# Group B softmax of a two-layer streaming encoder: a chained row minimum, a plain scale that ScalarE may do, and the factor 1/2 put into the output weights

## The chip, the cores and the metric

The kernel runs on one core of one Trainium2 chip. A core has TensorE (PE in the profile, with its weight loads as PEld), VectorE (DVE), ScalarE (ACT), GpSimd (POOL), SyncE (SP), which issues the DMAs, an on-chip memory (SBUF) that all of them read, and a smaller one (PSUM) that TensorE writes. The metric is device time in microseconds (us) for one execution, lower is better; a figure without further words is the median of three runs.

## The reference

Two layers of a streaming encoder, one inference step for 2048 prompt frames and 32 sample frames, model width 1024, all in fp32. What matters here is layer 0. One projection gives two attention groups; each group's output is multiplied by its own SiLU gate, the two are concatenated, and one output projection follows.

```python
def ab_output(oa, ob, ga, gb, w_out):
    y = jnp.concatenate([oa.reshape(b, t, -1) * jax.nn.silu(ga),
                         ob.reshape(b, t, -1) * jax.nn.silu(gb)], axis=-1)
    return y @ w_out

def attend(q, k, v, q_pos, k_pos, valid, bias_table, sinks):
    s = einsum(q, k) * (dh ** -0.5)
    if bias_table is not None: s = s + bias          # group B
    s = where(valid, s, -1e30)
    if sinks is not None:                            # group A
        m = maximum(max(s), sink); p = exp(s - m); p = p / (sum(p) + exp(sink - m))
    else:
        p = softmax(s)                               # group B
    return einsum(p, v)
```

Group A looks back two chunks of 64 frames, with 8 query heads on 2 key heads and a learned sink; group B looks back eight chunks, with 8 heads and a learned bias by distance. Layer 1 (projection, short convolution, linear recurrence, output projection) comes after all of layer 0. Of silu(g) = g * sigmoid(g) the kernel computes g * (1 + tanh(g/2)), which is twice silu(g). The missing factor 1/2 has to be applied somewhere, and this is one of the things that the change moves.

## The kernel before

Every large matrix product is done as three products of fp32r parts: a weight tile `wst` of 128x1024 is split into a rounded part `wh` and a rest `wl`, the activations into `r0h` and `r0l` (or `r1h`, `r1l`), and TensorE adds r0h*wh, r0l*wh and r0h*wl into one PSUM tile `acc`. These dense products are most of TensorE's work.

The order of all instructions is set when the program is built. The kernel holds its own list scheduler (`Sched`): each piece of work is a Python generator that yields a request `R(engines, inputs, rings, cost)`; the scheduler keeps an estimated time for each engine, gives a request to the engine that would finish it first by the costs written there, and records the instruction in that order. On the chip each engine then runs its list strictly in order and waits on semaphores. A request with several engines, such as ("V", "G"), lets the scheduler choose among VectorE (V), GpSimd (G) and ScalarE (A). Attention work has priority on TensorE; where none is ready, the dense products of `dense_P` (input projection) and later `dense_2` (output projection, then layer 1) fill in. So a change of one cost or of one instruction moves much that comes after it.

Layer 0 has three blocks of tokens. Attention for the tiles of a block runs between the dense products of the next ones; the last block's attention lies under the first third of the output projection, and the other output blocks wait for the key `("attention",)`.

A tile of group B attention has 128 queries and up to 640 keys, and goes through these steps, in the functions `soft`, `transp` and `evac_B`:

1. TensorE computes the scores into PSUM tiles `S` (two matmuls a bank, with the rounded query parts `qa` and `qb`). 640 keys don't fit into one bank of 512, so there are two banks of 320, that is two entries of `groups`.
2. VectorE runs one fused instruction for each bank (`reduce`; in the profile CUSTOM_DVE_ANT_0): it adds the bias, changes the sign, writes `pt` in SBUF and keeps the row minimum, which a second short instruction (DVE_READ_ACCUMULATOR2_ANT; in the built order both are named ISA) writes to a column of `nm`.
3. With two banks, a further VectorE instruction on two columns of 128x1 takes the smaller of the two minima (`nm<-nm`). There are 96 of them for prompt tiles and 8 for the sample.
4. ScalarE computes exp(-pt + nm) over all 640 columns, with the row sum into `ssm`; VectorE takes its reciprocal into `rr`.
5. VectorE or GpSimd multiplies `pt` by `rr` and by 0.5 (`pt<-pt,rr`).
6. TensorE transposes `pt` block by block into PSUM tiles `T`; ScalarE writes the rounded copy and VectorE the rest into `pp`; TensorE multiplies `pp` by the values `vt` into `O`; ScalarE and VectorE add the parts into `ot`, and a DMA writes it out.

Group A goes the same way with four heads beside each other; its fused instruction starts from the sink (operand `nsk`), so it has no step 3.

The output projection's weights (named "wo0" in `WSEQ`, 8 tiles for each of the 3 blocks) are split like all others, by `w_split`: `wh` on ScalarE or VectorE, `wl` on VectorE or GpSimd.

Of the kernel before, what the change touches and what calls it, by code (L numbers as in the profile page):

```python
# [11 lines left out]
AF = mybir.ActivationFunctionType  # L12
OP = mybir.AluOpType
# [42 lines left out]
def f32(ap):  # L56
    return ap.bitcast(F32)
# [341 lines left out]
def hybrid_kernel(ctx, tc, I, O):  # L399
# [85 lines left out]
    def w_split():  # L485
        for i in range(1, len(WSEQ)):
# [6 lines left out]
            s = wst.pop(i)  # L493
            if e == "A":
                A.copy(h, s)
            else:
                V.tensor_copy(h, s)
            e, _ = yield R(("V", "G"), [h], cost=(1.14, 2.3))
            ENG[e].tensor_tensor(l, s, f32(h), OP.subtract)
            wstr.release(s)  # L500
# [730 lines left out]
    def soft(run, np_, groups, out, sink=None):  # L1231
# [9 lines left out]

        def reduce(ps, pieces, o0):
            yield R("V", [ps] + ex)
            o = 0
            for i, (_, ks, bv, j) in enumerate(pieces):
                n = ks.stop - ks.start
                V.tensor_tensor_reduce(out=pt[:np_, o0 + o:o0 + o + n], in0=ps[:np_, o:o + n], in1=bv, scale=-1.0,
                                       scalar=BIG if sink is None else nsk[:np_, sink + j:sink + j + 1],
                                       op0=OP.add, op1=OP.min, accum_out=nm[:np_, j:j + 1])
                o += n  # L1250
            Sr.release(ps)
            left[0] -= 1
            if not left[0]:
                if run.bias is not None:
                    run.b_done()
                if sink is None and len(groups) == 2:
                    V.tensor_tensor(nm[:np_, 0:1], nm[:np_, 0:1], nm[:np_, 1:2], OP.min)
                if sink is not None:
                    V.tensor_tensor(r[:np_], sk[:np_, sink:sink + 4], nm[:np_], OP.add)
                sch.set(uid, sch.t["V"] + 0.13)  # L1260

        for gi, pieces in enumerate(groups):
# [5 lines left out]
            for qs, ks, _, _ in pieces:  # L1268
# [3 lines left out]
                o += n  # L1272
            spawn(reduce(ps, pieces, o0), PT)
            o0 += o
# [14 lines left out]
        n = sum(x[1] for x in out)  # L1289
        e, _ = yield R(("V", "G"), [r], cost=(0.06 + n * 0.00053, 0.1 + n * 0.00106))  # L1290
        for j, (o, w) in enumerate(out):
            x = pt[:np_, o:o + w]
            ENG[e].tensor_scalar(x, x, r[:np_, j:j + 1], 0.5, OP.mult, OP.mult)
        for g, t in ((nmr, nm), (smr, ss), (rr4, r)):
# [827 lines left out]
```

## Time and profile before

| what | value |
| --- | --- |
| median of 3 runs | 1827.37 us (1827.22 to 1828.31) |
| the profiled execution's own time | 1823.5 us |
| span of that execution, first to last instruction | 1821.7 us |
| TensorE busy | 1731.5 us, 95% of the span |
| VectorE busy | 1555.3 us, 85% |
| ScalarE busy | 996.5 us, 55% |
| GpSimd busy | 326.5 us, 18% |
| mean share of the full TensorE clock that was granted | 0.988 |
| first and last score minimum that is taken from two banks | 412.8 and 989.9 us |

The profile is of one execution, and its times count from the first instruction. Almost all instructions pass through one helper, so they all stand at line L101; the names of the tiles tell them apart (out<-in, buffer numbers left out). A busy time counts an instruction from its start to its end, and on TensorE and VectorE one starts before the one before it has ended, so the distance between two starts is what an instruction costs its engine. "Idle before" is the engine's idle time just before an instruction, with what ended it; gaps under 150 ns aren't counted.

### The profile page before, as it was taken

Reading aid. Unit: us, or ns where it says so; the run is one execution under the profiler, and the core shown is the slowest. Engines: PE = TensorE matmul, PEld = TensorE weight load, DVE = VectorE, ACT = ScalarE, POOL = GpSimd, SP = SyncE. Lnnn points to the kernel's source line nnn. Section 1 sums busy time; section 2 is a strip of 40 time slices with the busy share of each in tenths; the row PEclk is TensorE's granted clock in tenths of the full one; section 3 lists DMA queues with packets and bytes.
Section 4 is the critical chain, followed back from the end, with each engine's and each line's share of the span. In section 5 each row is a group of like instructions: output and inputs, shape, how many; then the busy total and the mean of one; then the engine's idle time right before and its main releaser. Section 6 shows DMA issues by size and latency. Waiting matters only on the chain.

```text
span 1821.7 us, 31694 instructions
## 1 busy us (share of the span) xinstructions
PE 1731.5 (95%) x11078; PEld 1671.8 (92%) x11078; DVE 1555.3 (85%) x3330; ACT 996.5 (55%) x2037; POOL 326.5 (18%) x284
## 2 busy tenths in 40 slices
PE   8999999999999999999998999998999999999995
PEld 7999999998999999899997999998999899999995
DVE  9899967899998779998988789899999988798843
ACT  4275543476666416665565344457753675447831
POOL 4332204323322233311222000000011000100002
PEclk8999999999999999999998999999999999999998
DMA  5788766888654368877764985684566735575376
GB/s 179 203 245 265 228 190 196 226 232 237 192 149 141 97 186 248 210 217 195 216 194 122 278 248 168 210 267 147 217 213 217 204 124 174 165 208 171 128 268 193
DMA packets 293576, 362.80 MB, mean 199 GB/s; under 512 B 36308, under 2 KB 244616, under 8 KB 293400
## 3 DMA queue, kind: packets, MB, share of 16 engines
q1 hardware_dynamic: 293416, 360.78, 66.5%
q8 instruction: 87, 1.43, 0.3%
q14 instruction: 73, 0.60, 0.1%
HBM read 255.77 MB, written 107.00 MB: 199 GB/s over the span
## 4 chain that ended last, share of the span: by engine, by line
PE 49%; DVE 29%; DMA 9%; ACT 6%; issue 4%; SPq 1%; POOL 1%; DVEq 0%; ACTq 0%; POOLq 0%
PE acc L101 35%; PE T L101 4%; PE O L101 4%; PE S L101 4%; DVE pt L101 3%; DVE ex L101 3%; DVE m L101 3%; DMA xr<-x2T 3%; DVE ss L101 2%; DVE ti L101 2%; DVE xs L101 2%; DVE s L101 2%; DVE pp L101 2%; DVE eti L101 1%; DVE wl L101 1%
## 5 line engine op out<-in xcount | busy, mean ns | idle before, releaser
L101 PE MATMUL acc<-r0h,wh 128*128 128x352 f32 (+2 forms) x1832 | 592.1, 323 | 6.7 <-ACT tzb L101 2.9
L101 PE MATMUL acc<-r0h,wl 128*128 128x352 f32 (+2 forms) x1832 | 592.2, 323 | 2.9 <-DMA wl<-wo1s 2.9
L101 PE MATMUL acc<-r0l,wh 128*128 128x352 f32 (+2 forms) x1832 | 592.5, 323 | 0.6 <-DVE r0l L101 0.5
L101 PEld LDWEIGHTS acc<-r0h,wh 128*128 128x128 f32 x1832 | 346.2, 189 | 9.3 <-ACT tzb L101 3.1
L101 PEld LDWEIGHTS acc<-r0h,wl 128*128 128x128 f32 x1832 | 346.3, 189 | 4.8 <-DMA wl<-wo1s 4.0
L101 PEld LDWEIGHTS acc<-r0l,wh 128*128 128x128 f32 x1832 | 346.4, 189 | 2.2 <-DVE r0l L101 1.2
L101 PE MATMUL acc<-r1h,wh 128*128 128x352 f32 (+1 forms) x864 | 277.5, 321 | 5.2 <-ACT tz L101 3.6
L101 PE MATMUL acc<-r1h,wl 128*128 128x352 f32 (+1 forms) x864 | 277.0, 321 | 1.6 <-DVE wl L101 1.6
L101 PE MATMUL acc<-r1l,wh 128*128 128x352 f32 (+1 forms) x864 | 276.9, 321 | 0.0
L101 ACT ACTIVATE pt<-pt,nm 128x256 f32<-128x256 f32 (+6 forms) x272 | 169.8, 627 | 61.2 <-DVE nm L101 59.3
L101 ACT CAST pp<-T 128x256 fp32r<-128x256 f32 (+4 forms) x314 | 134.0, 438 | 84.3 <-PE T L101 65.8
L101 PEld LDWEIGHTS acc<-r1h,wh 128*128 128x128 f32 x864 | 162.3, 188 | 6.4 <-ACT tz L101 4.5
L101 POOL TENSOR_SCALAR pt<-pt,rr 128x256 f32<-128x256 f32 (+4 forms) x142 | 100.2, 716 | 366.4 <-DVE rr L101 217.0
L101 PEld LDWEIGHTS acc<-r1h,wl 128*128 128x128 f32 x864 | 162.3, 188 | 1.9 <-DVE wl L101 1.9
L101 PEld LDWEIGHTS acc<-r1l,wh 128*128 128x128 f32 x864 | 162.3, 188 | 0.0
L101 PE MATMUL T<-ident,pt 128*128 128x128 f32 (+2 forms) x864 | 143.3, 274 | 18.0 <-DVE pp L101 10.2
L101 DVE TENSOR_TENSOR pp<-T,pp 128x256 fp32r<-128x256 f32 (+4 forms) x314 | 150.4, 496 | 7.9 <-ACT pp L101 6.0
L101 PE MATMUL O<-pp,vt 128*128 128x256 f32 (+3 forms) x728 | 135.9, 310 | 9.8 <-DVE pp L101 4.7
L101 PEld LDWEIGHTS T<-ident,pt 128*128 128x128 f32 (+2 forms) x864 | 101.7, 140 | 42.4 <-DVE pp L101 19.9
L101 DVE CUSTOM_DVE_ANT_0 pt<-S,bias 128x320 f32<-128x320 f32 (+2 forms) x240 | 108.8, 478 | 17.4 <-PE S L101 14.6
L101 PE MATMUL S<-kk,qa 128*128 128x320 f32 (+5 forms) x376 | 119.7, 333 | 3.8 <-DVE nm L101 3.3
L101 PEld LDWEIGHTS O<-pp,vt 128*128 128x128 f32 (+1 forms) x728 | 107.1, 193 | 16.0 <-DVE pp L101 6.1
(241 smaller groups left out, 3010.1 us busy)
## 6 DMA issues: line engine op xcount, KB each, us to landing
wst<-w_in SPq DMA_DIRECT2D x93, 512.0 KB, 4.4
wst<-wo_in SPq DMA_DIRECT2D x32, 512.0 KB, 5.6
wh<-w1s SPq DMA_DIRECT2D x32, 512.0 KB, 3.8
wl<-w1s SPq DMA_DIRECT2D x32, 512.0 KB, 4.6
wh<-wo1s SPq DMA_DIRECT2D x24, 512.0 KB, 3.9
wl<-wo1s SPq DMA_DIRECT2D x24, 512.0 KB, 4.7
kk<-kB SPq DMA_DIRECT2D x32, 320.0 KB, 4.8
vt<-vB SPq DMA_DIRECT2D x16, 640.0 KB, 4.8
```

Of the source, the lines that this page charges most:

```text
L101: r = fn(*a, **k)
```

## The change

Three edits:

- **The chained minimum.** In group B the second bank's fused instruction starts its minimum from the first bank's result (column 1 of `nm`, as a scalar operand) and writes column 0. The separate minimum of step 3 is gone. The second bank's instruction now waits for the first bank's minimum to be written.
- **The plain scale.** Step 5 multiplies by `rr` alone. Where one instruction covers the whole tile (group B), ScalarE may do it too, at an estimated cost of 0.197 us + n/1200.
- **The factor 1/2.** It goes into the split of the "wo0" tiles: `wh` is 0.5 times the weight, and `wl` is 0.5 times the weight minus `wh`, one fused VectorE instruction; GpSimd may no longer do it for these 24 tiles.

```diff
@@ w_split
+            half = WSEQ[i][0] == "wo0"
+            if half:
+                if e == "A":
+                    A.activation(h, s, AF.Copy, scale=0.5)
+                else:
+                    V.tensor_scalar(h, s, 0.5, None, OP.mult)
+                yield R("V", [h])
+                V.scalar_tensor_tensor(l, s, 0.5, f32(h), OP.mult, OP.subtract)
             else:
-                V.tensor_copy(h, s)
-            e, _ = yield R(("V", "G"), [h], cost=(1.14, 2.3))
-            ENG[e].tensor_tensor(l, s, f32(h), OP.subtract)
...
@@ soft
-        def reduce(ps, pieces, o0):
-            yield R("V", [ps] + ex)
+        def reduce(ps, pieces, o0, gi):
+            on = gi > 0 and sink is None
+            yield R("V", [ps] + ex + ([(uid, 0)] if on else []))
...
+                if sink is None:
+                    j = len(groups) - 1 - gi
                 V.tensor_tensor_reduce(out=pt[:np_, o0 + o:o0 + o + n], in0=ps[:np_, o:o + n], in1=bv, scale=-1.0,
-                                       scalar=BIG if sink is None else nsk[:np_, sink + j:sink + j + 1],
+                                       scalar=nsk[:np_, sink + j:sink + j + 1] if sink is not None else nm[:np_, 1:2] if on else BIG,
                                        op0=OP.add, op1=OP.min, accum_out=nm[:np_, j:j + 1])
...
-                if sink is None and len(groups) == 2:
-                    V.tensor_tensor(nm[:np_, 0:1], nm[:np_, 0:1], nm[:np_, 1:2], OP.min)
...
-        e, _ = yield R(("V", "G"), [r], cost=(0.06 + n * 0.00053, 0.1 + n * 0.00106))
+        e, _ = yield R(("V", "G", "A")[:3 if len(out) == 1 else 2], [r], cost=(0.06 + n * 0.00053, 0.1 + n * 0.00106, 0.197 + n / 1200.0))
...
-            ENG[e].tensor_scalar(x, x, r[:np_, j:j + 1], 0.5, OP.mult, OP.mult)
+            if e == "A":
+                A.activation(x, x, AF.Copy, scale=r[:np_, j:j + 1])
+            else:
+                ENG[e].tensor_scalar(x, x, r[:np_, j:j + 1], None, OP.mult)
```

Since the scheduler plans anew, the built order of every engine differs from there on. Three places show what moves. In the rows, the numbers at the names are buffers; `x3` is three equal instructions in a row.

VectorE, the first pair of banks in the program (in block 1). Before:

```order
L101 ISA pt_211,nm_216<-S_194,bias_207 128x320
L101 ISA nm_216 128x1
L101 ISA pt_211,nm_216<-S_195,bias_207 128x320
L101 ISA nm_216 128x1
L101 TENSOR_TENSOR nm_216<-nm_216 128x1
L101 TENSOR_TENSOR ot_214<-O_198,ot_214 64x512
```

And now:

```order
L101 ISA pt_211,nm_216<-S_194,bias_207 128x320
L101 ISA nm_216 128x1
L101 ISA pt_211,nm_216<-S_195,bias_207,nm_216 128x320
L101 ISA nm_216 128x1
L101 TENSOR_TENSOR ot_214<-O_198,ot_214 64x512
```

The minimum is gone, and the second bank's instruction reads `nm`. In all, 104 minima go; in 71 of the 104 pairs the second instruction stands right behind the first's minimum, and in the others something stands between.

ScalarE, the first such tiles of block 1 (exp of a tile, then the copies of transposed tiles). Before:

```order
L101 ACTIVATE pt_210,ssm_222<-pt_210,nm_218 128x640
L101 CAST pp_212<-T_196 128x2x128
L101 COPY ot_215<-O_198 64x512
L101 CAST pp_212<-T_197 128x3x128
L101 CAST pp_213<-T_196 128x3x128
L101 ACTIVATE pt_211,ssm_223<-pt_211,nm_219 128x640
```

And now:

```order
L101 ACTIVATE pt_210,ssm_222<-pt_210,nm_218 128x640
L101 ACTIVATE pt_210<-pt_210,rr_226 128x640
L101 CAST pp_212<-T_197 128x2x128
L101 CAST pp_212<-T_196 128x3x128
L101 COPY ot_215<-O_198 64x512
```

A scale by `rr` now stands in ScalarE's list, ahead of copies out of `T`. Of the scales of 640 columns GpSimd had 57 and VectorE 39; now GpSimd has 28, VectorE 43 and ScalarE 25. With the shorter ones ScalarE has 33.

TensorE, a pair of group B tiles of one of the last heads of the last block, from the last tile's first transposes to the end of `O` (the dense products between them are `acc`). Before:

```order
L101 MATMUL T_196<-ident,pt_209 128x128 x3
L101 MATMUL acc_159<-r0l,wh_121 128x324
L101 MATMUL acc_159<-r0h,wl_124 128x324
L101 MATMUL acc_159<-r0h,wh_121 128x324
L101 MATMUL acc_159<-r0l,wh_121 128x324
L101 MATMUL O_198<-pp_212,vt_206 128x2x128 x4
L101 MATMUL acc_159<-r0h,wl_124 128x324
L101 MATMUL acc_159<-r0h,wh_121 128x324
L101 MATMUL acc_159<-r0l,wh_121 128x324
L101 MATMUL acc_159<-r0h,wl_124 128x324
L101 MATMUL O_198<-pp_212,vt_206 128x2x128 x4
L101 MATMUL O_198<-pp_212,vt_206 128x256 x2
```

And now:

```order
L101 MATMUL T_196<-ident,pt_209 128x128 x3
L101 MATMUL O_198<-pp_212,vt_206 128x2x128 x4
L101 MATMUL acc_158<-r0h,wh_121 128x352
L101 MATMUL acc_158<-r0l,wh_121 128x352
L101 MATMUL acc_158<-r0h,wl_124 128x352
L101 MATMUL acc_158<-r0h,wh_121 128x352
L101 MATMUL O_198<-pp_212,vt_206 128x2x128 x4
L101 MATMUL O_198<-pp_212,vt_206 128x256 x2
```

Four dense matmuls between the transposes and the first `O` are gone from here and come later. Over the program TensorE's 11061 matmuls stay the same; the last one of attention was the 6291st and is now the 6163rd, so 128 dense matmuls that stood before the end of attention now stand behind it. Nearly all of that is in the attention of the last block.

Beyond these, the 24 splits of "wo0" tiles use the new instructions. VectorE now does all 24 rests, and over all weights GpSimd has 37 rests of 128x1024 and had 39.

More of the change, by code (lines that the diff above doesn't have):

```diff
@@ L493, in w_split @@
             s = wst.pop(i)
-            if e == "A":
-                A.copy(h, s)
-            else:
-                V.tensor_copy(h, s)
-            e, _ = yield R(("V", "G"), [h], cost=(1.14, 2.3))
-            ENG[e].tensor_tensor(l, s, f32(h), OP.subtract)
+            half = WSEQ[i][0] == "wo0"
[6 more added lines that the diff above has]
+                V.scalar_tensor_tensor(l, s, 0.5, f32(h), OP.mult, OP.subtract)
+            else:
+                if e == "A":
+                    A.copy(h, s)
+                else:
+                    V.tensor_copy(h, s)
+                e, _ = yield R(("V", "G"), [h], cost=(1.14, 2.3))
+                ENG[e].tensor_tensor(l, s, f32(h), OP.subtract)
             wstr.release(s)
@@ L1251, in reduce @@
             Sr.release(ps)
+            sch.set((uid, gi), sch.t["V"])
             left[0] -= 1
@@ L1272, in soft @@
                 o += n
-            spawn(reduce(ps, pieces, o0), PT)
+            spawn(reduce(ps, pieces, o0, gi), PT)
             o0 += o
@@ L1289, in soft @@
         n = sum(x[1] for x in out)
-        e, _ = yield R(("V", "G"), [r], cost=(0.06 + n * 0.00053, 0.1 + n * 0.00106))
+        e, _ = yield R(("V", "G", "A")[:3 if len(out) == 1 else 2], [r], cost=(0.06 + n * 0.00053, 0.1 + n * 0.00106, 0.197 + n / 1200.0))
         for j, (o, w) in enumerate(out):
             x = pt[:np_, o:o + w]
-            ENG[e].tensor_scalar(x, x, r[:np_, j:j + 1], 0.5, OP.mult, OP.mult)
+            if e == "A":
+                A.activation(x, x, AF.Copy, scale=r[:np_, j:j + 1])
+            else:
+                ENG[e].tensor_scalar(x, x, r[:np_, j:j + 1], None, OP.mult)
         for g, t in ((nmr, nm), (smr, ss), (rr4, r)):
```

## The prediction

> **What bounds the kernel now.** I read the page's totals first, then the stretches of time in the last block's attention, where the built order moves most. The columns of a stretch are its length, then for each engine the busy time and the instructions, then the granted TensorE clock, the DMA share and GB/s.
>
> ```profile
> PE 1731.5 (95%) x11078; PEld 1671.8 (92%) x11078; DVE 1555.3 (85%) x3330; ACT 996.5 (55%) x2037; POOL 326.5 (18%) x284
> ...
> 840.00:900.00 60.00, 59.48 (x416) 56.84 (x416) 54.37 (x170) 35.98 (x84) 10.90 (x8) 1.00 0.74 207
> 900.00:960.00 60.00, 57.02 (x396) 54.13 (x395) 53.69 (x157) 35.31 (x79) 18.19 (x11) 1.00 0.73 196
> 960.00:1000.00 40.00, 34.66 (x212) 31.89 (x213) 32.71 (x89) 23.07 (x53) 10.04 (x6) 0.87 0.40 123
> 1000.00:1040.00 40.00, 40.00 (x256) 40.00 (x255) 28.12 (x37) 15.82 (x30) 0.94 (x1) 1.00 0.85 257
> ```
>
> TensorE is the bound: 1731.5 of 1821.7 us, and nothing in this change takes a matmul away. So the change can only touch the 90.2 us in which TensorE is idle, and time that its clock is low. VectorE comes next: 54 of 60 us in these stretches, so a delay there is soon a delay of TensorE. From 960 to 1000 TensorE loses 5.3 us idle and has 0.87 of its clock, another 40 x 0.13 = 5.2 us; right after attention it is full.
>
> Next, what TensorE's idle time waits for between 780 and 1000 us (groups of instructions there), and the start and end of the `O` matmuls in the whole program (rows of the tile `pp`):
>
> ```profile
> L101 PE MATMUL T<-ident,pt 128*128 128x128 f32 (+1 forms) x277 | 47.1, 273 | 6.7 <-DVE pp L101 4.2 <-DMA vt<-vBs 1.1 <-POOL pt L101 0.9
> L101 PE MATMUL O<-pp,vt 128*128 128x256 f32 (+2 forms) x273 | 43.3, 292 | 3.2 <-DVE pp L101 1.8 <-DMA vt<-vBs 1.3
> L101 PE MATMUL S<-kk,qa 128*128 128x320 f32 (+1 forms) x106 | 36.7, 354 | 0.6 <-DVE nm L101 0.6
> ...
> L101 PE MATMUL O<-pp,vt x728: 193/283/582, 95.3 to 1002.0; 128*128 128x256 f32 x141, 128*128 128x512 f32 x31, 128*128 128x64 f32 x8, 32*128 32x64 f32 x2
> ```
>
> That is 10.5 us in 220 us, 6.0 of it ended by VectorE's writing of `pp` and 0.6 by `nm`. Then I looked at what stood ahead of `pp` on VectorE, at the longest such wait (timeline of VectorE, GpSimd, TensorE and ScalarE from 957 us: start, length, instruction):
>
> ```profile
> 957.66 0.48 DVE L101 CUSTOM_DVE_ANT_0 pt<-S,bias 128x320 f32<-128x320 f32 x1
> 958.07 0.08 DVE L101 DVE_READ_ACCUMULATOR2_ANT nm<- 128x1 f32 x1
> 958.18 1.75 DVE L101 TENSOR_TENSOR nm<-nm 128x1 f32<-128x1 f32 x1
> 959.86 0.87 DVE L101 TENSOR_TENSOR pp<-T,pp 128x256 fp32r<-128x256 f32 x2
> ...
> 957.56 2.36 POOL L101 TENSOR_TENSOR wl<-wst,wh 128x1024 fp32r<-128x1024 f32 x1
> ...
> 960.32 0.44 PE L101 MATMUL T<-ident,pt 128*128 128x128 f32 x2 [1.66 <-DVE pp L101]
> ...
> 960.03 0.83 ACT L101 ACTIVATE pt<-pt,nm 128x640 f32<-128x640 f32 x1 [3.11 <-DVE nm L101]
> ```
>
> A minimum of one column takes 1.75 us. It ends at 959.93, as GpSimd's 2.36 us instruction does (959.92): it waited for it. `pp` waits behind it, and TensorE idles 1.66 us for `pp`. The fused instruction ran through the same GpSimd instruction in its usual 0.48 us. The chain of waits, by line, says how often this decides (100 and 200 us):
>
> ```profile
> by line: PE acc L101 24.1%; DVE pt L101 12.0%; DVE pp L101 9.8%; DVE ss L101 7.8%; DVE ot L101 6.2%; PE T L101 5.8%; issue 5.7%; PE S L101 5.1%; PE O L101 5.0%; DMA oT<-ot 4.6%; DVE nm L101 4.0%; DVE xt L101 3.3%; PE misc L101 1.5%; DVE sr
> ...
> by line: PE acc L101 19.8%; PE O L101 9.5%; DVE pt L101 9.2%; DMA vt<-vBs 8.5%; PE T L101 8.0%; PE S L101 7.3%; DMA xt<-zT 6.1%; DVE ot L101 5.6%; DVE pp L101 4.4%; DVE nm L101 3.7%; issue 3.5%; DVE r0l L101 2.0%; DVE xt L101 1.8%; DVE s L1
> ```
>
> The first is 400 to 500 us, the second 800 to 1000 us: `nm` has 4.0 and 7.4 us on the chain, 11.4 together.
>
> **The change, part by part.** The minimum undisturbed, and the groups by form:
>
> ```profile
> 437.05 0.08 DVE L101 DVE_READ_ACCUMULATOR2_ANT nm<- 128x1 f32 x1
> 437.17 0.16 DVE L101 TENSOR_TENSOR nm<-nm 128x1 f32<-128x1 f32 x1
> 437.24 0.15 DVE L101 RECIPROCAL rr<-ssm 128x1 f32<-128x1 f32 x1
> ...
> L101 DVE TENSOR_TENSOR nm<-nm x104: 147/159/1815, 412.8 to 989.9; 128x1 f32<-128x1 f32 x96, 32x1 f32<-32x1 f32 x8
> ...
> L101 DVE TENSOR_TENSOR nm<-nm 128x1 f32<-128x1 f32 x96 | 30.8, 321 | 3.3
> L101 DVE CUSTOM_DVE_ANT_0 pt<-S,amask,nsk 128x256 f32<-128x256 f32 x120 | 51.6, 477 | 2.9 <-PE S L101 2.5
> L101 DVE CUSTOM_DVE_ANT_0 pt<-S,bias 128x256 f32<-128x256 f32 x8 | 3.3, 414 | 0.0
> L101 DVE TENSOR_TENSOR wl<-wst,wh 128x1024 fp32r<-128x1024 f32 x86 | 110.8, 1288 | 2.8 <-ACT wh L101 0.8
> L101 DVE TENSOR_SCALAR pt<-pt,rr 128x640 f32<-128x640 f32 x39 | 24.5, 633 | 0.7
> L101 POOL TENSOR_SCALAR pt<-pt,rr 128x640 f32<-128x640 f32 x57 | 55.2, 970 | 237.1 <-DVE rr L101 146.1 <-ACT pp L101 39.0 <-PE O L101 13.3
> L101 ACT ACTIVATE pt<-pt,nm 128x640 f32<-128x640 f32 x96 | 79.9, 832 | 37.4 <-DVE nm L101 35.8 <-DVE pp L101 1.2
> ```
>
> The minimum, removed: from the end of the bank's own work (437.05) to the next start (437.24) it costs VectorE 0.19 us, of which 0.12 is waiting for the result just written. 104 x 0.19 = 19.8 us. Its mean of 321 ns against a median of 159 adds 96 x 0.16 = 15.6 us of waits like the one above.
>
> The Trainium skill, page SBUF — State Buffer, section "Who interferes with whom", gives the rule: a VectorE instruction with two SBUF inputs is shut out for the whole of a GpSimd instruction that reads SBUF and started first, one with at most one SBUF input is not. The trace agrees on both (1.75 us for `nm<-nm`, 0.48 us for the fused one). By that rule the wait isn't lost but passed on where the next VectorE instruction too has two SBUF inputs; the built order has that after 17 of the 104 pairs (`ot<-ot`), while 77 are followed by reads of `T` or `O` in PSUM, so by the rule a sixth of the 15.6 us would return, 2.6 us of VectorE time.
>
> The second bank's new operand: no row shows it, the nearest are the fused instruction with a column operand (`nsk`) and without, both of 256 columns: 477 - 414 = 63 ns, 6.6 us for 104. The new wait for the first bank's minimum is bounded by 0 (33 pairs have other work between) and the 0.12 us above: 71 x 0.12 = 8.5 us at most, and I take all of it. Queued behind it are `pp` and `ot`, as behind the minimum before. So an undisturbed adjacent pair gains just 0.19 - 0.06 - 0.12 = 0.01 us; nearly all the gain is in the disturbed ones.
>
> The scale: one product fewer gives nothing that a row shows; I take 0, between 0 and the whole gap of the rows above. 29 scales of 640 columns leave GpSimd (970 ns each); 4 of them go to VectorE, 4 x 0.63 = 2.5 us, and 25 to ScalarE. Their price there lies between 0.63 (VectorE's) and 0.97 us (GpSimd's); I take 0.83, exp over the same 640 columns. With the shorter ones 33 x 0.83 = 27 us over 960 us, on an engine busy 35 of 60: hidden by its idle 25, and if that cover were gone `pp` and then TensorE would wait up to 0.83 us each. TensorE's 0.9 us for GpSimd's `pt` I count as gone.
>
> The half in the weights: 2 rests more on VectorE, 2 x 1.29 = 2.6 us, from about 960 us on, where VectorE is busy 28.12 of 40 us while TensorE is full. Between 0 and 2.6; I take 0. No DMA is added or removed; those of attention are issued earlier, along with it.
>
> The moved cover: 128 dense matmuls of 0.155 us each (40.00 us for 256 at the end of attention) = 19.8 us of TensorE's work no longer lie under attention but behind it. This by itself costs nothing if attention does end 19.8 us sooner.
>
> The sum, on the chain: the minima give 11.4 us. About 30 of them can have stood there, between 11.4/1.75 = 7 and 11.4/0.16 = 71; each gives back 0.063 + 0.12 x 71/104 = 0.145, together 4.3. Of the remaining 7.1 us I count half as kept, since the stages beside it on the chain (`pt` 9.2%, `vt` DMA 8.5%, `xt` DMA 6.1%, `ot` 5.6%) stay and will be late next: 3.6. With 0.9 for GpSimd's `pt`: 4.5 us. The profiled execution's own 1823.5 would become 1819.0. That execution was 3.9 us quicker than the median of 1827.37, so the median becomes **1822.9 us**.
>
> **The rivals.**
>
> *Nothing to measure.* The minima's waits lie beside `pp`, `ot` and `vt` waits that end as late; then 0 to 2 us, about 1826.5. For it speaks that TensorE's idle from 780 to 1000 is just 10.5 us, and that VectorE's undisturbed gain is so small. Against it, that 1.66 us of idle at 960.32 hang on one minimum.
>
> *Out of cover, slower.* The built order takes 19.8 us of dense work out of the last block's attention. VectorE gets less: that stretch has 56 of the 104 pairs (48 prompt tiles and 8 sample ones), 56 x (0.32 - 0.145) = 9.8 us. If VectorE or the `vt` DMAs set the pace, attention ends 10 us sooner, not 20, and TensorE idles the difference: +10, 1837 us. It decides if the last `O`, now at 1002.0, starts later than 1002 - 19.8 = 982 us; each us beyond costs one. For it speaks VectorE at 54 of 60; against it, that the chain there also has waits that the change takes away.
>
> *The low clock goes as well.* If TensorE idles less from 960 to 1000, the 5.2 us of lost clock there are saved too: 1822.9 - 5.2 = 1817.7. Against it: that tail has still less cover now. The Trainium skill, page TensorE: Matmul & The Clock Gate, section "What's actually happening", says that an idle window of about 3.4 us halves the clock until a busy one has passed; the 0.87 here agrees with that, but no row here shows its threshold.
>
> *ScalarE in the way.* If a quarter of the 27 us of scales delays copies of `T` that TensorE waits for, +7: 1834 us. VectorE's `pp` waits for just those copies; ScalarE's 25 idle us of 60 speak against it.
>
> **How the numbers follow.** What a measurement here can tell from no change is 0.2%, 3.7 us: under 1823.7 is faster, over 1831 slower. Forecast 0.44 (own range 1819 to 1825; 0.36 of it counts as faster, 0.08 as same), low clock gone 0.10, nothing 0.23, out of cover 0.18, ScalarE 0.05. So faster 0.46, same 0.31, slower 0.23. The lower end: 11.4 + 0.9 + 5.2 = 17.5 us would be 1810, of which I keep 1811. The upper end is short of 1837, at 1835, which leaves part of the out-of-cover case outside.
>
> **What would show it.** In the changed profile: no `nm<-nm`; the second bank's instruction near 0.54 us where the first's is 0.48, with a gap of 0.12 us ahead when adjacent; no 1 to 2 us waits in front of exp while GpSimd splits weights; 25 scales of 640 columns on ScalarE near 0.83 us; the last `O` between 976 and 984 us; TensorE idle some 5 us less before it, and unchanged after it. The forecast is wrong if the last `O` comes at 985 us or later, if the `T` and `O` idle after 780 us is over 10 us as before, or if new idle time appears in layer 1, whose order changes too without any cause in the steps above.

## The result, and the profile after

The changed kernel takes 1839.38 us (median of 7 runs, 1837.35 to 1844.25) where the kernel before takes 1828.31 (7 runs beside it): a ratio of 1.0067, 95% interval 1.005 to 1.0084. That is 11 us slower by the medians and 12 by the ratio. The profiled execution has a span of 1841.5 us, so it lies a little above the median; that of before lay a little below.

The page's totals of the changed kernel:

```profile
PE 1742.0 (95%) x11078; PEld 1676.2 (91%) x11078; DVE 1538.8 (84%) x3231; ACT 1017.1 (55%) x2071; POOL 349.6 (19%) x245
```

VectorE has 16.5 us less to do, as meant. GpSimd has 39 instructions fewer and yet 23.1 us more. The stretches around the end of attention, and then the groups of TensorE between 780 and 1000 us with the extent of the `O` matmuls:

```profile
840.00:900.00 60.00, 56.23 (x393) 52.79 (x394) 49.81 (x154) 40.00 (x93) 9.95 (x5) 1.00 0.72 192
900.00:960.00 60.00, 58.84 (x409) 53.83 (x408) 53.36 (x168) 42.75 (x97) 14.32 (x8) 1.00 0.76 211
960.00:1000.00 40.00, 34.30 (x235) 32.90 (x233) 30.99 (x69) 21.72 (x47) 3.28 (x2) 0.96 0.61 186
1000.00:1040.00 40.00, 39.50 (x229) 39.12 (x230) 28.02 (x35) 16.73 (x30) 0.00 (x0) 0.92 0.89 271
...
L101 PE MATMUL T<-ident,pt 128*128 128x128 f32 (+2 forms) x288 | 49.3, 272 | 6.7 <-POOL pt L101 4.7 <-DVE pp L101 1.7
L101 PE MATMUL O<-pp,vt 128*128 128x256 f32 (+3 forms) x290 | 45.4, 288 | 0.7 <-DVE ot L101 0.6
...
L101 PE MATMUL O<-pp,vt x728: 192/283/507, 95.9 to 984.6; 128*128 128x256 f32 x140, 128*128 128x512 f32 x31, 128*128 128x64 f32 x8, 32*128 32x64 f32 x3
```

Attention ends at 984.6 us, 17.4 sooner, and the waits for VectorE's `pp` have shrunk. But `T` idles as long as before: it now waits for GpSimd's `pt`. And right behind attention there is a new wait, in the dense products (TensorE's group from 900 to 1030 us, before and then after):

```profile
L101 PE MATMUL acc<-r0h,wh 128*128 128x352 f32 (+1 forms) x155 | 50.5, 326 | 0.0
```

```profile
L101 PE MATMUL acc<-r0h,wh 128*128 128x352 f32 (+1 forms) x156 | 51.9, 333 | 5.9 <-ACT r0h L101 5.9
```

Only 9.7 us of TensorE's work lie between the end of attention and this wait, which lasts from 994.3 to 1000.2 us; in the chain of waits ahead of it stand two DMAs, `xr<-oT` with 5.8 and `zT<-s` with 5.2 us. Together, idle time and lost clock from 960 to 1040 us come to 11.0 us in the rows above (6.2 idle, 4.8 of clock), where the kernel before lost 10.5.

`T` over the whole program, before and then after:

```profile
L101 PE MATMUL T<-ident,pt 128*128 128x128 f32 (+2 forms) x864 | 143.3, 274 | 18.0 <-DVE pp L101 10.2 <-DVE rr L101 2.6 <-DVE pt L101 2.0
```

```profile
L101 PE MATMUL T<-ident,pt 128*128 128x128 f32 (+1 forms) x864 | 145.8, 276 | 23.0 <-POOL pt L101 12.3 <-DVE pp L101 8.9 <-DVE rr L101 0.4
```

The waits for GpSimd's `pt` went from 1.4 us (the fourth cause in the kernel before, which the row leaves out) to 12.3; others became shorter, so that `T` idles 5.0 us more. The groups by form say why. First the 256-column scale on GpSimd before (the 640-column one, 970 ns, stands in the prediction), then the changed kernel:

```profile
L101 POOL TENSOR_SCALAR pt<-pt,rr 128x256 f32<-128x256 f32 x74 | 38.7, 542 | 66.6 <-DVE rr L101 21.6 <-ACT sr L101 13.0 <-PE O L101 8.4
```

```profile
L101 POOL TENSOR_SCALAR pt<-pt,rr 128x256 f32<-128x256 f32 x75 | 73.0, 988 | 76.7 <-DVE rr L101 30.9 <-PE S L101 9.6 <-DMA zT<-s 7.3
L101 POOL TENSOR_SCALAR pt<-pt,rr 128x640 f32<-128x640 f32 x28 | 56.9, 2032 | 221.8 <-DVE rr L101 114.4 <-PE S L101 65.1 <-PE O L101 18.9
L101 DVE CUSTOM_DVE_ANT_0 pt<-S,bias,nm 128x320 f32<-128x320 f32 x96 | 52.7, 549 | 12.0 <-PE S L101 1.8 <-DVE nm L101 1.0 <-PE acc L101 0.2
L101 DVE CUSTOM_DVE_ANT_0 pt<-S,bias 128x320 f32<-128x320 f32 x96 | 46.4, 483 | 10.8 <-PE S L101 10.3
L101 DVE TENSOR_SCALAR pt<-pt,rr 128x640 f32<-128x640 f32 x43 | 23.6, 552 | 1.1
L101 ACT ACTIVATE pt<-pt,rr 128x640 f32<-128x640 f32 x25 | 20.8, 830 | 3.6 <-DVE rr L101 3.5
```

With one product instead of two, VectorE's scale of 640 columns is a little shorter (633 to 552 ns); GpSimd's takes twice as long: 970 to 2032 ns, and 542 to 988 for 256 columns. That is 28 x 1.06 + 75 x 0.45 = 63 us of GpSimd's time.

To see where the loss lies I laid the runs beside each other by TensorE's work: every matmul counts with its kind's usual start-to-start time in the kernel before (the value that 30% of them stay under), and the table says how many us later than the kernel before a profiled run has done the same amount. Another choice of that usual time moves these figures by up to about 1 us. Each column is one execution: the two spans of before and after lie 19.8 us apart where the medians lie 11 apart, so some 8 us of the column "after" belong to the two executions that were profiled. The names E1, E2 and so on are the runs below.

| work done, us | time before | after | E1 | E2 | E3 | E8 | E13 |
| --- | --- | --- | --- | --- | --- | --- | --- |
| 120 | 140.4 | +3.5 | +0.3 | +3.3 | +1.2 | -0.3 | +0.8 |
| 200 | 230.2 | +7.8 | +4.4 | +5.1 | +1.6 | +0.2 | +1.0 |
| 640 | 725.6 | +10.8 | +4.3 | +9.1 | +1.9 | +0.0 | -4.0 |
| 880 | 1015.5 | +12.4 | +5.2 | +14.1 | +2.8 | +4.0 | -4.9 |
| 1000 | 1142.9 | +16.7 | +8.7 | +14.1 | +4.0 | +21.8 | +0.2 |
| 1200 | 1363.4 | +17.3 | +5.7 | +10.8 | +0.2 | +17.2 | -2.6 |
| 1240 | 1403.6 | +17.2 | +5.6 | +10.6 | +20.8 | +38.3 | -2.7 |
| 1560 | 1743.9 | +17.1 | +5.2 | +10.7 | +18.2 | +34.8 | -3.3 |
| 1600 | 1786.7 | +20.4 | +8.0 | +11.2 | +20.4 | +35.0 | -2.4 |

The changed kernel loses 8 us before 240 us, where group A and the short tiles of group B with one bank run and there is no chained minimum; 5 us more by the end of attention; 4 to 5 us just after 1100 us; and 3 at the very end. The last is in layer 1, where the change has no instruction. Near the one after 1100 us the change has just splits of "wo0" weights, and the new form of `wl` takes as long there as the old one, 1.20 and 1.22 us. The wait after 1100 us, in the chain of waits of the changed kernel, and the group of TensorE that waits there (before from 1098 to 1116 us, after from 1109 to 1130), is this:

```profile
1109.88 0.49 DVE sacc L101
1110.37 1.13 DVE wl L101
1111.50 1.30 DVE ss L101
...
1112.82 0.80 ACT sq L101
...
1113.64 1.34 DVE ss L101
1114.99 0.43 DVE sacc L101
1115.42 0.45 DVE ss L101
...
1116.29 1.22 PE misc L101 x2
1117.51 12.53 PE acc L101 x63
```

```profile
L101 PE MATMUL misc<-xs,onesr 128*128 128x352 f32 x2 | 0.9, 426 | 2.2 <-ACT xs L101 1.1 <-DVE xs L101 1.1
```

```profile
L101 PE MATMUL misc<-xs,onesr 128*128 128x352 f32 x2 | 1.2, 660 | 4.2 <-DVE xs L101 4.2
```

In the changed kernel a `sacc` and a `wl` stand on VectorE ahead of two of the sums of squares of the next norm (`ss`); in the kernel before a `wl` and a `sacc` stand there too, but behind the last of these sums. TensorE idles 4.2 us at a stretch, where the kernel before idles twice, 1.1 us each. In the changed kernel the clock is halved for a stretch behind it (the seventh number); the last row is the kernel before behind its second wait:

```profile
1112.00:1116.00 4.00, 0.12 (x1) 0.00 (x0) 3.11 (x5) 3.18 (x6) 0.00 (x0) 0.99 1.14 339
1116.00:1120.00 4.00, 3.71 (x12) 3.44 (x13) 3.93 (x7) 0.70 (x2) 0.00 (x0) 0.50 0.65 210
1120.00:1124.00 4.00, 4.00 (x19) 4.00 (x18) 0.91 (x3) 0.80 (x2) 0.00 (x0) 0.65 0.25 98
...
1106.00:1110.00 4.00, 3.90 (x24) 3.90 (x25) 3.29 (x8) 0.56 (x1) 0.00 (x0) 1.00 0.43 131
```

So 2 us more of idle time cost about 5: 2.0 idle, and by the two rows 4 x 0.50 + 4 x 0.35 = 3.4 of lost clock. The Trainium skill, page TensorE: Matmul & The Clock Gate, section "What's actually happening", puts the clock at half after an idle window of about 3.4 us; 4.2 us of idle with half the clock behind it agree. But the length of a single wait doesn't decide it here, and the measurement differs from that figure: behind waits of about 2 us the clock went either way. The same wait of `g<-xs,gh` for `xs` is 1.99 us in the kernel before, at 1272.5 us, and 1.97 in the changed one, at 1289.4; the 4 us behind it, before and then after:

```profile
1272.50:1276.50 4.00, 3.97 (x25) 3.97 (x26) 3.81 (x7) 3.61 (x5) 0.00 (x0) 1.00 1.00 342
```

```profile
1289.40:1293.40 4.00, 3.97 (x15) 3.97 (x16) 3.07 (x4) 2.52 (x3) 0.00 (x0) 0.58 1.01 347
```

### The profile page after: what moved, and what is told of

The parts are those of the page before. It is cut to its first block, busy times and chain, and to the rows that moved or that the text cites. A ratio compares the mean times of both kernels' runs of the same rounds, so it can differ in the third digit from the quotient of the medians.

```text
span 1841.5 us, 31587 instructions
## 1 busy us (share of the span) xinstructions
PE 1742.0 (95%) x11078; PEld 1676.2 (91%) x11078; DVE 1538.8 (84%) x3231; ACT 1017.1 (55%) x2071; POOL 349.6 (19%) x245
## 4 chain that ended last, share of the span: by engine, by line
PE 27%; DVE 17%; DMA 7%; ACT 6%; issue 3%; POOL 1%; SPq 0%; DVEq 0%; ACTq 0%; POOLq 0%
PE acc L101 21%; DVE m L101 3%; DVE ex L101 3%; DMA xr<-x2T 2%; DVE ti L101 2%; PE T L101 2%; DVE xs L101 2%; PE O L101 2%; PE S L101 2%; DVE eti L101 1%; DMA wl<-wo1s 1%; DVE r L101 1%; PE g L101 1%; DMA x2T<-m 1%; DVE ss L101 1%
## 5 line engine op out<-in xcount | busy, mean ns | idle before, releaser
L101 POOL TENSOR_SCALAR pt<-pt,rr 128x256 f32<-128x256 f32 (+4 forms) x111 | 137.8, 1252 | 314.4 <-DVE rr L101 151.6
L101 PE MATMUL T<-ident,pt 128*128 128x128 f32 (+1 forms) x864 | 145.8, 276 | 23.0 <-POOL pt L101 12.3
L101 DVE TENSOR_TENSOR pp<-T,pp 128x256 fp32r<-128x256 f32 (+4 forms) x314 | 151.2, 497 | 12.9 <-ACT pp L101 11.2
L101 PEld LDWEIGHTS T<-ident,pt 128*128 128x128 f32 (+1 forms) x864 | 99.6, 139 | 54.2 <-DVE pp L101 19.6
L101 PE MATMUL O<-pp,vt 128*128 128x256 f32 (+2 forms) x728 | 133.9, 308 | 4.6 <-DVE ot L101 2.5
L101 ACT ACTIVATE m<-acc,vec 128x352 f32<-128x352 f32 (+2 forms) x89 | 48.8, 548 | 145.8 <-PE acc L101 140.3
```

The lines of the kernel that those rows point to most:

```text
L101: r = fn(*a, **k)
```

## The experiments

Theory A: GpSimd's one-operation scale costs the time. Theory B: the new order of the instructions costs it, at places that have nothing to do with the change. Most runs below hold an order: the planner books the instructions of the one kernel, and others are issued in their places, so that TensorE's and SyncE's lists are the same one for one and only the edited instructions differ.

**E1: the changed kernel, GpSimd's scale with two operations.**

```diff
-                ENG[e].tensor_scalar(x, x, r[:np_, j:j + 1], None, OP.mult)
+                if e == "G":
+                    G.tensor_scalar(x, x, r[:np_, j:j + 1], 1.0, OP.mult, OP.mult)
+                else:
+                    ENG[e].tensor_scalar(x, x, r[:np_, j:j + 1], None, OP.mult)
```

> The changed kernel, in the same order on every engine, but GpSimd's scale has its second operation back (times 1.0); VectorE's scale keeps one operation. Theory A (the form of GpSimd's scale costs the time: 128x640 went from 970 to 2032 ns and 128x256 from 542 to 988 ns, and T waited 12.3 us in all for GpSimd's pt): the scales are back near 970 and 542 ns, the lag of about 8 us that opens between 100 and 240 us goes, and the time is 1825 to 1831, a ratio of 0.998 to 1.002 to the kernel before. Theory B (the new order costs it: 128 dense matmuls behind attention, another order in layer 1): the GpSimd durations fall, but the time stays within 3 us of 1839, ratio 1.005 or more. A mixture would lie at 1832 to 1836.

Measured 1.004 (1.0022 to 1.0058), 1830.4 us beside 1822.2. The scale is short again and the new waits are gone (groups of GpSimd by form, and of TensorE over the whole program):

```profile
L101 POOL TENSOR_SCALAR pt<-pt,rr 128x640 f32<-128x640 f32 x28 | 26.1, 933 | 244.5 <-DVE rr L101 116.3 <-PE S L101 76.5 <-PE O L101 20.6
...
L101 PE MATMUL T<-ident,pt 128*128 128x128 f32 (+1 forms) x864 | 143.3, 275 | 16.8 <-DVE pp L101 14.1 <-POOL pt L101 1.0 <-DVE rr L101 0.4
```

The form is worth 0.27% here, some 5 us; the two intervals, of E1 and of the changed kernel, just overlap, and the rows above and E2 carry it. It is not all: 0.4% stays, and of the 7.8 us that the table has at 230 us, 4.4 stay.

**E2: the kernel before, GpSimd's scale with one operation.**

```diff
-            ENG[e].tensor_scalar(x, x, r[:np_, j:j + 1], 0.5, OP.mult, OP.mult)
+            if e == "G":
+                G.tensor_scalar(x, x, r[:np_, j:j + 1], None, OP.mult)
+            else:
+                ENG[e].tensor_scalar(x, x, r[:np_, j:j + 1], 0.5, OP.mult, OP.mult)
```

> The kernel before, in its own order, but GpSimd's scale is a single product; the factor 1/2 is left out there, so the rows that GpSimd scales come out twice as large. Theory A: GpSimd's 57 scales of 640 columns go to about 2.0 us and the 74 of 256 columns to about 1.0 us, T waits for GpSimd's pt by 10 us and more, and the time is 1836 to 1845 (the kernel before has 57 long ones where the changed one has 28, so the loss may be larger than the 11 us seen). Theory B: 1828 to 1831, no difference to speak of.

Measured 1.0059 (1.0041 to 1.0077), 1833.4 beside 1822.2: 11 us from this edit alone, somewhat below the expected range's lower end of 1836. The same two groups:

```profile
L101 POOL TENSOR_SCALAR pt<-pt,rr 128x640 f32<-128x640 f32 x57 | 115.1, 2022 | 193.5 <-DVE rr L101 113.1 <-ACT pp L101 32.4 <-PE T L101 20.1
...
L101 PE MATMUL T<-ident,pt 128*128 128x128 f32 (+2 forms) x864 | 146.7, 276 | 31.1 <-POOL pt L101 17.0 <-DVE pp L101 6.7 <-DVE pt L101 4.1
```

Theory A holds in both orders: 11 us here, where 57 long scales are on GpSimd, some 5 in the changed order with 28.

**E3: the kernel before with the chained minimum alone**, planned anew: the part of the change in `reduce`, nothing else of it.

```diff
-                                       scalar=BIG if sink is None else nsk[:np_, sink + j:sink + j + 1],
+                                       scalar=nsk[:np_, sink + j:sink + j + 1] if sink is not None else nm[:np_, 1:2] if on else BIG,
...
-                    V.tensor_tensor(nm[:np_, 0:1], nm[:np_, 0:1], nm[:np_, 1:2], OP.min)
```

> The kernel before with the chained minimum alone (the scale keeps two operations and its two engines, the half stays in the scale). The prediction's reasoning (the minima's waits stand on the chain for 11.4 us, a third of it kept): 1824 to 1826. The rival that these waits lie beside others that end as late: 1827 to 1829. Out of cover, slower because the order changes: above 1832.

Measured 1.0095 (1.0076 to 1.0114), 1840.2 us: a miss for both readings of the minimum, and within the third, above 1832 because the order changes. The table shows it within 4 us of the kernel before until 1363 us, and then 20 us late by 1424, in layer 1. TensorE's group over the whole program, before and in E3, and two stretches of E3:

```profile
L101 PE MATMUL acc<-r1h,wh 128*128 128x352 f32 (+1 forms) x864 | 277.5, 321 | 5.2 <-ACT tz L101 3.6 <-DVE ex L101 1.7
```

```profile
L101 PE MATMUL acc<-r1h,wh 128*128 128x352 f32 (+1 forms) x864 | 280.2, 324 | 20.6 <-ACT r1h L101 16.4 <-ACT tz L101 2.2 <-DVE ex L101 1.7
...
1390.00:1400.00 10.00, 8.34 (x50) 7.80 (x48) 9.66 (x16) 3.16 (x7) 0.00 (x0) 1.00 0.28 105
1400.00:1410.00 10.00, 0.00 (x0) 0.00 (x0) 9.99 (x15) 1.56 (x2) 0.00 (x0) 0.51 0.53 145
```

One wait of 16.4 us for `r1h`, while VectorE is busy almost without a gap, in an order of its own. No instruction of group B's softmax is near.

**E4: E1 without ScalarE's share**, planned anew.

```diff
-        e, _ = yield R(("V", "G", "A")[:3 if len(out) == 1 else 2], [r], cost=(0.06 + n * 0.00053, 0.1 + n * 0.00106, 0.197 + n / 1200.0))
+        e, _ = yield R(("V", "G"), [r], cost=(0.06 + n * 0.00053, 0.1 + n * 0.00106))
```

> The changed kernel with two operations on GpSimd and no scale on ScalarE (VectorE and GpSimd only). If ScalarE's 25 scales relieve the other two, this is slower than the same kernel with them by 1 to 4 us; if they stand in the way of the copies of T, it is faster by 2 to 7 us; if they are hidden, as the prediction has it, within 2 us.

Measured 1.0014 (1.0003 to 1.0025). Faster than E1 by 0.26%, by which ScalarE's share would be in the way; but the order differs too, so that this tells nothing by itself. E11 and E13 hold the order.

**E5: the chained minimum alone, order held.** In the kernel before, both reductions stay in their places with a new starting operand and column, and the minimum is booked but not issued:

```diff
-                    V.tensor_tensor(nm[:np_, 0:1], nm[:np_, 0:1], nm[:np_, 1:2], OP.min)
+                    sch.book("V", "tensor_tensor", [nm[:np_, 0:1]], [nm[:np_, 0:1], nm[:np_, 1:2]], (), {})
```

> The kernel before in its own order, held on every engine: only the second bank's reduction goes on from the first's minimum, and the 104 minima are gone from VectorE. The previous run of the minimum alone came out 1.0095 with a 16.4 us wait for r1h in layer 1, where the edit has no instruction. Theory B (that loss was the new order): with the order held the edit saves the minima's waits, 0 to 7 us, the forecast's share is 3.6, ratio 0.996 to 1.000, and TensorE has no wait of 16 us in layer 1. Rival (the chained minimum itself is what costs time, by a wait for its operand or by VectorE's pace): 1.005 or more with the order held too.

Measured 0.9977 (0.9963 to 0.9992): 4.2 us faster. The same edit as in E3, 1.2% apart: theory B.

**E6: all but ScalarE's share and GpSimd's form, order held.** E5 with this and the half in the out weights (GpSimd, where the old plan gives it a `wl` of these, halves `wst` in an instruction of its own first):

```diff
-            ENG[e].tensor_scalar(x, x, r[:np_, j:j + 1], 0.5, OP.mult, OP.mult)
+            ENG[e].eng.tensor_scalar(x, x, r[:np_, j:j + 1], None if e == "V" else 1.0, OP.mult, *(() if e == "V" else (OP.mult,)))
+            sch.book(e, "tensor_scalar", [x], [x, r[:np_, j:j + 1]], (), {})
```

> The kernel before in its own order, held, with the whole change but ScalarE's share and GpSimd's one-operation form: chained minimum, VectorE's scale with one operation, GpSimd's with two (times 1.0), the half in the out weights. Theory B: like the run with the minimum alone, 0.996 to 1.000; VectorE's single product adds 0 to 3 us of gain (633 to 552 ns on 39 scales of 640 columns is 3.2 us of VectorE's time). If the parts of the change other than GpSimd's form cost time in themselves: above 1.002.

Measured 0.999 (0.9973 to 1.0008). VectorE's shorter scale and the half in the weights add nothing that shows over E5 (the intervals overlap).

**E7 and E8: other orders of the kernel before.** No operation is changed, only a constant of the planner by 0.4 and 1%:

```diff
-        return 0.1 + n * 0.00223
+        return 0.1 + n * 0.00224
```

> The kernel before with no operation changed: only a planning constant (GpSimd's price per column of a two-input operation, 0.00223 to 0.00224 us) is moved by half a per cent, which gives another order of the same work. If the order alone is worth as much as the change: the time moves by 5 to 20 us in either direction, with single waits of TensorE of several us in layer 1. If the time hardly depends on such details: within 2 us of the kernel before.

> As the run before it, with another planning constant (ScalarE's fixed price 0.104 to 0.105 us): a second order of the same work. Same two readings: 5 to 20 us in either direction if the order alone matters that much, within 2 us if it doesn't.

Measured 1.021 (1.0187 to 1.0234) and 1.0196 (1.0171 to 1.0221), 38 and 35 us slower by nothing but the order, more than the 5 to 20 us that were expected. Two waits carry it, here in E8 over the whole program:

```profile
L101 PE MATMUL acc<-r1h,wh 128*128 128x352 f32 (+1 forms) x864 | 279.7, 324 | 20.1 <-ACT r1h L101 16.4 <-ACT tz L101 2.0 <-DVE ex L101 1.7
L101 PE MATMUL g<-r0h,wl 128*128 128x352 f32 (+1 forms) x32 | 11.4, 357 | 15.4 <-DVE wl L101 14.8 <-ACT m L101 0.6
```

The first is E3's wait to the tenth; the second is 14.8 us for a weight's `wl` where the kernel before idles 0.0.

**E9: five forms of the scale on GpSimd**, in turn, in lines 1326, 1328, 1330, 1332 and 1334 (E6 otherwise).

```diff
...
+            elif f == 0:
+                G.eng.tensor_scalar(x, x, c, None, OP.mult)
+            elif f == 1:
+                G.eng.tensor_scalar(x, x, c, 1.0, OP.mult, OP.mult)
+            elif f == 2:
+                G.eng.tensor_scalar(x, x, c, 0.0, OP.mult, OP.add)
+            elif f == 3:
+                G.eng.tensor_scalar(x, x, 1.0, c, OP.mult, OP.mult)
+            else:
+                G.eng.tensor_scalar(x, x, 0.5, None, OP.mult)
```

> The kernel before in its own order (chained minimum, half in the out weights, one operation on VectorE), where GpSimd's scales take five forms in turn, each on a line of its own: times the column alone; column times 1.0; column plus 0.0; 1.0 times the column; and a constant 0.5 alone, which leaves the normalisation out on those tiles. One look, for the duration of each form at 128x640 and 128x256. If a single operation is what is slow on GpSimd: the first and the fifth near 2.0 and 1.0 us, the other three near 0.97 and 0.54. If the second product is what matters and not the number of operations: column plus 0.0 is slow too. If a column as the last operand is what matters: the fourth differs from the second, and the fifth is fast.

The groups of GpSimd by form:

```profile
L1326 POOL TENSOR_SCALAR pt<-pt,rr 128x640 f32<-128x640 f32 x12 | 25.0, 2082 | 51.0 <-DVE rr L101 27.9 <-PE acc L101 19.4 <-PE O L101 1.9
L1334 POOL TENSOR_SCALAR pt<-pt 128x640 f32<-128x640 f32 x11 | 20.2, 1833 | 53.0 <-ACT pt L101 52.7 <-DMA bias<-rel_in 0.3
...
L1330 POOL TENSOR_SCALAR pt<-pt,rr 128x640 f32<-128x640 f32 x11 | 12.4, 1131 | 49.9 <-DVE rr L101 33.4 <-PE O L101 11.2 <-DVE ot L101 5.3
L1328 POOL TENSOR_SCALAR pt<-pt,rr 128x640 f32<-128x640 f32 x12 | 11.1, 924 | 29.6 <-DVE rr L101 23.8 <-ACT pp L101 5.4 <-PE T L101 0.4
L1332 POOL TENSOR_SCALAR pt<-pt,rr 128x640 f32<-128x640 f32 x11 | 10.7, 973 | 25.8 <-DVE rr L101 20.7 <-PE acc L101 4.2 <-PE T L101 0.9
```

It is the number of operations: any second one, a product or a sum, about halves the time; a constant alone is as slow as a column alone. What GpSimd does differently inside isn't shown. (The time of this one run isn't used: its fifth form doesn't wait for `rr`.)

**E10: the changed kernel's operations in the order of before**, ScalarE's share left away. E6 with

```diff
-            ENG[e].eng.tensor_scalar(x, x, r[:np_, j:j + 1], None if e == "V" else 1.0, OP.mult, *(() if e == "V" else (OP.mult,)))
+            ENG[e].eng.tensor_scalar(x, x, r[:np_, j:j + 1], None, OP.mult)
```

> The kernel before in its own order, held, with the changed kernel's operations: chained minimum, the half in the out weights, one operation on VectorE and on GpSimd; only ScalarE's share is left away. By theory A the parts add up: 0.999 of the run with two operations on GpSimd plus the 0.0059 that the single one cost in this order, 1.003 to 1.007, 1830 to 1838 us. If the chained minimum and the shorter VectorE scale give GpSimd's delay room to hide: 0.999 to 1.002.

Measured 1.0062 (1.0041 to 1.0083), 0.7% above E6, from which it differs only in GpSimd's form: the parts add up.

**E11: E1 with ScalarE's scales issued on VectorE, order held.**

```diff
-                A.activation(x, x, AF.Copy, scale=r[:np_, j:j + 1])
+                V.eng.tensor_scalar(x, x, r[:np_, j:j + 1], None, OP.mult)
+                sch.book("A", "activation", [x], [x, r[:np_, j:j + 1]], (x, x, AF.Copy), {"scale": r[:np_, j:j + 1]})
```

> The changed kernel with two operations on GpSimd (1.004 when run), in its own order, held; the scales that its plan gives to ScalarE are issued at the same places on VectorE instead. If ScalarE's share stands in the way of the copies of T and is what lies between 1.004 and the 1.0014 of the kernel without it: 1.000 to 1.003. If the order that came with it is what costs: 1.004 or above, since VectorE gets 25 x 0.55 = 14 us more work.

Measured 1.012 (1.0093 to 1.0146), slower than E1's 1.004. In E11 `T` waits longer for VectorE's `pp`, 20.8 us instead of 14.1 (in an execution with a mean clock of 0.935, where the other three had 0.983 to 0.988):

```profile
L101 PE MATMUL T<-ident,pt 128*128 128x128 f32 (+1 forms) x864 | 144.9, 277 | 24.2 <-DVE pp L101 20.8 <-POOL pt L101 0.9 <-DVE pt L1307 0.7
```

So E4's 0.26% can't be had by giving these scales to VectorE. This doesn't clear ScalarE by itself, since VectorE gets 33 scales on top, the 25 long ones and 8 shorter.

**E12: E1 with the minimum taken apart again, order held.** Both reductions start from `BIG`, and behind the second (booked as the chained one):

```diff
+                if on:
+                    V.eng.tensor_tensor(nm[:np_, 0:1], nm[:np_, 0:1], nm[:np_, 1:2], OP.min)
```

> The changed kernel with two operations on GpSimd, in its own order, held; the minimum is taken apart again (both banks start from the constant, and a minimum of one column stands behind the second). If the chained minimum is worth in this order what it is worth in that of before (0.23%): 1.005 to 1.008 where the chained one has 1.004. If it is worth nothing here: 1.003 to 1.005. If the chained form costs: below 1.003.

Measured 1.005 (1.003 to 1.0071), against 1.004: the intervals overlap, so what the chained minimum is worth in the changed order stays open.

**E13: ScalarE's share in the order of before.** E6, with every second of GpSimd's 57 scales of 640 columns issued on ScalarE:

```diff
+            if e == "G" and w == 640 and n_ % 2:
+                A.eng.activation(x, x, AF.Copy, scale=r[:np_, j:j + 1])
```

> The kernel before in its own order, held, with the whole change and two operations on GpSimd; of the 57 scales of 640 columns on GpSimd every second one (29) is issued on ScalarE at the same place. ScalarE in the way (the rival of the prediction): 29 x 0.83 = 24 us of scales delay copies of T, a quarter of it is 6 us, ratio 1.002 to 1.005. ScalarE's share hidden, as the prediction had it: like the run without it, 0.997 to 1.001; then the rest of the loss is the order's.

Measured 0.9962 (0.9944 to 0.998), 1818.2 beside 1824.5 us. A little better than expected, and the lowest median of all: nearly the whole change, with two operations on GpSimd, in the old order. (GpSimd still makes the rest of 3 "wo0" tiles, and the other scales stay on the engines of the old plan.) ScalarE's scales (by form) and TensorE's `T` group:

```profile
L1320 ACT ACTIVATE pt<-pt,rr 128x640 f32<-128x640 f32 x29 | 24.2, 833 | 6.2 <-DVE rr L101 6.0
...
L101 PE MATMUL T<-ident,pt 128*128 128x128 f32 (+2 forms) x864 | 143.0, 274 | 15.5 <-DVE pp L101 9.4 <-DVE pt L1322 3.3 <-DVE rr L101 1.1
```

**E14 and E15: two further orders of E1**, by the planner's constants of E7 and E8, the second being

```diff
-            c = (0.104 if all(str(x.space).endswith("SB") for x in ins[:1]) else 0.067) + n / 1200.0 + 0.093 * ...
+            c = (0.105 if all(str(x.space).endswith("SB") for x in ins[:1]) else 0.067) + n / 1200.0 + 0.093 * ...
```

> The changed kernel with two operations on GpSimd, no operation changed, planned with GpSimd's price per column at 0.00224 instead of 0.00223 us. If the orders are a scatter of which the one of before is a good draw: between 1.000 and 1.025, away from 1.004 by 5 us or more in either direction. If the change's rules give orders that are alike: 1.002 to 1.006.

> As the run before it, with ScalarE's fixed price at 0.105 instead of 0.104 us. Same two readings: away from 1.004 by 5 us or more if orders scatter, 1.002 to 1.006 if the change's orders are alike.

Measured 1.0078 (1.005 to 1.0107) and 1.0011 (0.9991 to 1.003). The same operations in three orders give 1.0011, 1.004 and 1.0078. Of E15 the difference to E1 is 5 us, of E14 7; the intervals of these two don't overlap, so the orders do scatter.

## Why the prediction was wrong

The measured 0.67% comes apart in three: the change with two operations on GpSimd in the order of before, -0.38% (E13); from there to E1, -0.38 to +0.40, so +0.78% for the order, which engine gets which scale included; from E1 to the changed kernel, 0.40 to 0.67, so +0.27% for GpSimd's form. In us, about -7, +14 and +5. The first carries some 0.2% of uncertainty and each of the others, as a difference of two ratios, some 0.25%; E13 has 29 scales of 640 columns on ScalarE where the plan has 25.

**The step that failed first: "The scale: one product fewer gives nothing that a row shows; I take 0, between 0 and the whole gap of the rows above".** The bounds had no loss in them. No row before showed a one-operation scale on GpSimd, which was a reason to leave room for a loss; the term measured 1.06 us for each 640 columns and 0.45 for 256, 11 us of the time in the old order (E2). "TensorE's 0.9 us for GpSimd's `pt` I count as gone" came out as 4.7 us in the same stretch, 780 to 1000 us.

**The step that failed second, and weighed more: the new order had a price of 0.** It was named only as what would make the forecast wrong, "new idle time in layer 1, whose order changes too without any cause in the steps above", and had neither a term nor a rival nor a chance. The moved cover was looked at, and was to cost nothing if attention ends 19.8 us sooner. It ended 17.4 us sooner, but TensorE then ran out of work for 5.9 us, with the clock halved behind: the forecast's "unchanged after it" failed. The same wait for `r0h` stands in E1 (5.9 us), E4 (6.2) and E14 (6.7), and there is none in the kernel before, E5, E6, E13 and E15. It isn't the whole price of the order: E4 has it and measured 1.0014. What was not asked is how the time depends on the order as such. Eight orders were run; the seven others all come out above that of before, from 0.1% (E15, which can't be told from no change) to 2.1%, though five of them hold operations that are cheaper. A new plan that costs nothing is here the unlikely case.

**What held.** The minima are worth what was forecast: 3.6 us, and E5 measured 4.2, with an interval of 1.5 to 6.8. The path isn't shown as well as the size: TensorE's idle time in `T` and `O` between 400 and 1010 us went from 23.8 us only to 22.3 in E5. The new operand costs 549 - 483 = 66 ns (forecast 63).

Not shown is that a sixth of the minima's waits, 2.6 us, would be passed on to the next instruction. In E5's order 13 minima were followed directly by an `ot<-ot` (the 17 are of the changed order). Behind the one of them that had waited, at 440.7 us, `ot<-ot` took 0.84 us where it had taken 0.41; the other 12 stayed within 0.01 us. The 48 `ot<-ot` of 64x256 do take 2.3 us more in sum (the groups of VectorE by form, before and in E5), but 2.1 us of that stand in a single one, at 464.8 us, with no minimum that waited ahead of it. It began 0.03 us before a `wl` of GpSimd in the kernel before and took 0.42 us; in E5 it began 0.16 us behind that `wl` and took 2.51 us. For who is shut out, the rule of the Trainium skill, page SBUF — State Buffer, section "Who interferes with whom", agrees with both.

```profile
L101 DVE TENSOR_TENSOR ot<-ot 64x256 f32<-64x256 f32 x48 | 24.4, 507 | 0.8
```

```profile
L101 DVE TENSOR_TENSOR ot<-ot 64x256 f32<-64x256 f32 x48 | 26.7, 556 | 0.8
```

ScalarE's scales take 830 ns (forecast 0.83), and its share is hidden or better: E13 is 0.28% below E6, though that difference is near what the two intervals allow, and E11 shows what VectorE would pay instead. The half in the weights costs nothing that shows (E6). So the forecast of -4.5 us is near E13's -7, in part by luck: between E6 and E13 ScalarE's share gave perhaps 5 us, for which the forecast had 0. For the kernel that came of the new plan it was wrong.

**The rivals.** "Out of cover, slower" gave 1837 us and the measured time is near it, mostly by luck. Its deciding point, a last `O` after 982 us, was passed by only 2.6 us, which by its own rule is worth 2.6 us. TensorE did run out of work, for the 5.9 us above, but with the lost clock this cost as much as the tail of attention had cost before (11.0 and 10.5 us), so that it doesn't explain the loss. "ScalarE in the way" is refuted by E13 for the old order; for the changed order no run isolates it. "The low clock goes as well" came true from 960 to 1000 us (0.87 to 0.96) and was given back behind it (1.00 to 0.92). What the forecast said there of the 0.87, that it agrees with an idle window of 3.4 us, doesn't follow: the longest single wait of TensorE in that stretch was 1.67 us, at 968.1 us.

**Still open:** which rows of the changed order cost all of its 0.78%. The waits at 1000 and after 1100 us are named above; the loss of E1 between 185 and 230 us and from 700 to 930 was not followed to one instruction.

## What to carry to other kernels

An operand or operation that becomes simpler still is another form of the instruction: price it on each engine that may get it, and where no row shows that form, let the bounds include a loss. Where a planner fixes the order, hold the order to learn what an edit is worth, and count the new order as a term of its own, which for a kernel whose order is already a good one is more likely a loss than a gain (here in all seven new orders). After a replan look through the whole program for single long waits, not just around the edit; laying two traces beside each other by work done finds them.

## What the runs showed of the hardware

A scale on GpSimd with one operation, fp32 in SBUF, takes about twice as long as one with two: 2082 and 1833 ns against 924 to 1131 at 128x640 (E9). VectorE shows nothing like it (552 ns with one, 633 with two). And 2 us more of idle time at the wrong place can cost 5, by the granted clock: it was 0.50 in the 4 us behind idle stretches of 4.2 and 5.9 us of the changed kernel. Behind stretches of about 2 us it went either way, 1.00 after 1.99 us in the kernel before and 0.58 after 1.97 in the changed one; what decides between these isn't shown.
